# Rotation on the engine that is through first, bias rows first in the queue, attention over half of the dense steps, output products in another order: a four-layer decoder trunk on one core

## The chip, the core and the metric

The kernel runs on one core of a Trainium2 chip. A core has a matrix engine (TensorE, PE in the profile; its weight loads are PEld), two elementwise engines (VectorE, DVE; ScalarE, ACT), a programmable one (GpSimd, POOL) and an engine that here only issues transfers (SyncE, SP). Each works through its own list of instructions in order and waits on semaphores where it needs another's result. The metric is the device time of one execution in microseconds (us).

## The reference

The input is 256 tokens of 1024 numbers. Four layers follow each other. Layer i has a token mixer of kind i mod 3, so the kinds are A, B, C, A, and behind it a SwiGLU block of inner width 2816. Each of the two ends with `x <- LN(alpha*x + f(x))`, in float32.

- Mixer A: attention over a window of 128 tokens, 16 query heads on 4 key heads, with a bias on the projection and on the output, and a learned sink that joins the softmax's denominator.
- Mixer B: three groups of dilated attention with projections of their own, merged by their softmax denominators.
- Mixer C: causal attention in blocks of 256. At 256 tokens there is only the own block, so it is plain causal attention.

All queries and keys are rotated by position in the first 16 of their 64 numbers:

```
x1, x2 = xf[..., :half], xf[..., half:ROT_DIM]
return concatenate([x1 * c - x2 * s, x2 * c + x1 * s, xf[..., ROT_DIM:]], axis=-1)
```

## The kernel before

**Numbers.** Each float32 value is split in two float16 parts, and a product is made of three matmuls: high by high, high by low, low by high (`mm3`, L293 to L295, its three lines name nearly all matmuls of the page). Weights come from memory as float32 in pieces of 128 x 1024 (`raw`, four buffers). ACT makes a piece's high part (`whi`, L229), DVE its low part (`wlo`, L221). Four pieces are one chunk of 512 columns over 1024 rows, and five chunks can be alive at a time. Each of the 412 ring pieces passes this way once.

**One mixer layer.** The tokens are two tiles t of 128. A projection chunk and one token tile take eight steps (k = 0 to 7) of three matmuls into a PSUM bank `acc`, of which there are three. In mixer A a matmul of ones by the row `abias` (L300) adds the bias behind step 4. Then ACT copies the bank to SBUF (`qkv`, L864 in mixer A, L924 in B and C), POOL rotates the first 16 numbers of each head in four operations (L408 to L411), PE transposes the result against `ident` (L304), and ACT and DVE split it into `qkh` and `qkl` (L310, L314). There are 44 such rotations: 6 in each of the layers 0 and 3, 24 in layer 1, 8 in layer 2.

Attention runs in items, each for one token tile and one or two pairs of heads. An item has four kinds of steps: scores on PE with the row minimum on DVE (L521, into `s` and `mn`) and the exponential on ACT (L530); transposes of `s` and the split into `ph` and `pl`; products with the values into `pv`; and, for a group of four heads, the normalisation on DVE (L599, L601, into `oy`), a transpose and the split into `oth` and `otl`. POOL copies the sinks into `s` (L506).

The output product has steps of three matmuls over k for each token tile t and column half h, into one bank per (h, t). Two steps (k = 2q, 2q+1) need the normalised output of four heads. The LayerNorm of a token tile (L653 to L688; POOL takes a power, L680) follows the last product of its two halves, and its result is transposed for the next block.

**What sets the order.** The order of PE, ACT, DVE and POOL is written by a planner that runs while the kernel is built. It holds a time T for every engine and adds an assumed cost for each operation given out. `do(engine, us, dep, ...)` puts an operation into the engine's list when the planner's time has come to `dep`. A weight piece is handed to ACT when the planner believes that it has landed: `T["DMA"] + 2.0` (L257). `drive` (L342) mixes dense steps and attention steps: as long as the done share of attention is below the done share of the first `part` of the dense steps, it takes an attention step whose inputs are there by plan, two at most in a row. `part` is `A_PART`, `B_PART` or `C_PART` (L1064). A dense step of the output product is taken when its heads are collected by plan. SP's order comes from the framework, not from this planner.

**The start.** The eight first loads (x and the four pieces of chunk 0) go out on SP. POOL sends the positions, the sinks and the raw bias `araw`. `bias_parts` (L1022) makes the bias's high part on ACT and its low part on DVE, and POOL sends both as rows into `abias`. Before chunk 1 DVE and ACT make the angles' sine.

Of the kernel before, what the change touches and what calls it, by code (L numbers as in the profile page):

```python
# [18 lines left out]
P = 128  # L19
SEQ, D = 256, 1024  # L20
DEPTH = 4
NT = SEQ // P
# [21 lines left out]
def trunk(ctx, tc, a, out):  # L44
    nc = tc.nc
    ctx.enter_context(tc.manual_schedule(engines={getattr(mybir.EngineType, e) for e in ("PE", "Activation", "DVE", "Pool")}))
    pool = lambda name, bufs, **kw: ctx.enter_context(tc.tile_pool(name=name, bufs=bufs, **kw))
    RING, RAWS = 5, 4
    const = pool("const", 1)
    raw_p = pool("raw", RAWS)  # L50
    w_p = pool("w", RING)
# [32 lines left out]
    big0 = big.tile([P, NFB, SEQ], F16, name="htl").rearrange("p f s -> p (f s)").bitcast(F32)  # L84
    stage = [big0[:, :1024], big0[:, 1024:2048]] + [
        big.tile([P, NK, SEQ], F16, name=n).rearrange("p f s -> p (f s)").bitcast(F32) for n in ("oth", "otl")]
    for h in range(2):
        for t in range(NT):
            nc.sync.dma_start(X[t][:, h * 512:h * 512 + 512], a["x"][t * P:(t + 1) * P, h * 512:h * 512 + 512])
            i = 2 * h + t  # L90
            nc.sync.dma_start(stage[i], a["w_a"][0, 0][:, 1024 * i:1024 * i + 1024])
    nc.gpsimd.dma_start(pos_i, a["positions"].rearrange("(t p) -> p t", p=P))
    nc.gpsimd.dma_start(inv, a["inv"].partition_broadcast(P))
    nc.gpsimd.dma_start(sinks, a["a_sinks"].partition_broadcast(P))
    nc.gpsimd.dma_start(araw, a["a_bias"].rearrange("j (p c) -> p j c", p=P))

# [132 lines left out]
    def feed_one():  # L231

        c = ring["now"]
        if c is None:
            if ring["alive"] == RING:
                return False
            src = next(weights, None)
            if src is None:
                return False
            c = ring["now"] = new_w(*src)  # L240
            loaded.append(c)
        i = c["next"]
        c["next"] += 1
        until(lambda: raws[0] < NEVER)
        T["DMA"] = max(T["DMA"], raws.pop(0)) + 1.45
        raws.append(NEVER)
        slot[0] += 1
        number = slot[0]
        r = raw_p.tile([P, 1024], F32, name="raw")
        nc.sync.dma_start(r, c["src"][:, 1024 * i:1024 * i + 1024])  # L250

        def last(end):

            raws[RAWS - 1 - (slot[0] - number)] = end
        if c["next"] == len(c["ready"]):
            ring["now"] = None
        piece(c, i, r, T["DMA"] + 2.0, last)  # L257
        return True

    slot = [0]  # L260
# [138 lines left out]
    def rope(y, n, t, nh, dep, then):  # L399

        def turn():
            t1 = two.tile([P, 8, ROT], F32, name="rope1")[:, :nh]
            t2 = two.tile([P, 8, ROT], F32, name="rope2")[:, :nh]
            cb = cc[:, t:t + 1, :].to_broadcast([P, nh, ROT])
            sb0 = ss[:, t:t + 1, :h8].to_broadcast([P, nh, h8])
            sb1 = ss[:, t:t + 1, h8:].to_broadcast([P, nh, h8])
            e = nc.gpsimd
            e.tensor_tensor(t1, y[:, :, :ROT], cb, op=OP.mult)  # L408
            e.tensor_tensor(t2[:, :, :h8], y[:, :, h8:ROT], sb0, op=OP.mult)  # L409
            e.tensor_tensor(t2[:, :, h8:], y[:, :, :h8], sb1, op=OP.mult)  # L410
            e.tensor_tensor(y[:, :, :ROT], t1, t2, op=OP.add)  # L411
        do("POOL", 2.2, dep, turn, then)

    def transposed(y, t, n, dst, key):

# [376 lines left out]
    def hbuf(name):  # L792
        return big.tile([P, NFB, SEQ], F16, name=name).rearrange("p f s -> p (f s)").bitcast(F32)

    def finish(li, att, dense, oT, part, may_load=lambda: True, bias=None):

        PS, w = {}, []
        cell, load, half, ln = layer_norm(2 * li, lambda: [two.tile([P, 4, SEQ], F16, name=n) for n in ("qkh1", "qkl1", "qkh2", "qkl2")])

        def o(t):  # L800
            steps = []
            for k, h in [(2 * q + e, h) for q in range(NK // 2) for h in range(2) for e in range(2)]:
                if True:
                    def step(k=k, h=h):
                        if not w:
                            w.extend([next_w(), next_w()])
                        out_steps(PS, oT, NK, w[h], h, t, [k])[0]()
                        if bias is not None and k == 0:
                            add_row(PS[h, t][0], bias[:, 512 * h:512 * h + 512])
                    steps.append((step, lambda k=k: att.collected.get((t, k // 2), NEVER)))  # L810
            return steps
        steps = [(f, None) for f in dense]
        for t in range(NT):
            steps += o(t) + [(lambda t=t: ln(t, PS), None)]
        drive(att, steps, part, len(dense), may_load, load)
        done(2)
        return cell
# [18 lines left out]
    def mixer_a(li, j, cell):  # L836
# [60 lines left out]
            done(2)  # L897
        oT = new_ot()
        dense = chunk_steps(XT, evac(2))
        return finish(li, Attention(items(0) + items(1), oT), dense, oT, A_PART, bias=abias[:, 1536:])  # L900

    def mixer_bc(li, cell, ng):

# [118 lines left out]
    def bias_parts():  # L1022
        nc.scalar.activation(aparts[:, 0], araw, AF.Copy, scale=WS)
        nc.vector.scalar_tensor_tensor(aparts[:, 1], araw, WS, aparts[:, 0], op0=OP.mult, op1=OP.subtract)
        bias_rows(0, nc.gpsimd)

    def first_chunk(XT, evac):

        c = new_w(*next(weights))
        c["next"] = 4  # L1030
        land = [3.6, 5.2, 6.0, 7.6, 8.4, 10.0, 10.8, 12.4]
        spin(6)
        wait(land[0])
        transpose_x(0, XT, 0)
# [15 lines left out]
        for i in (2, 3):  # L1050
            piece(c, i, stage[i], land[1 + 2 * i])
        until(lambda: c["ready"][3] is not None)
        bias_parts()
        do("DVE", 2.2, 0.0, angles)
        T["ACT"] += 2.0
        ring["on"] = True
# [4 lines left out]
            f()  # L1061
        done()

    A_PART, B_PART, C_PART = 0.75, 0.95, 0.85  # L1064
    cell = {"XT": first_xt}
    for li in range(DEPTH):
        kind, j = li % 3, li // 3
# [94 lines left out]
```

## Time and profile before

| what | us |
|---|---|
| median of three runs | 1269.06 |
| lowest and highest of them | 1265.8, 1271.94 |
| the profiled execution's own time | 1272.32 |
| its span, first to last instruction | 1270.5 |
| PE busy | 1240.2 (98%) |
| DVE busy | 878.8 (69%) |
| ACT busy | 668.9 (53%) |
| POOL busy | 131.1 (10%) |

A busy PE isn't a PE at its peak: matmuls overlap, so a row of 0.38 us for 512 columns can follow the one before it by 0.22 us. PEclk is the granted clock as a share of the full 2.4 GHz, over the stretch. In a row of waits, the name behind the arrow is what came last by the profile; where that engine had long been done, it was another.

### The profile page before, as it was taken

How to read it: one execution, taken by the hardware profiler on the slowest of the kernel's cores; microseconds unless marked ns; L12 is line 12 of the kernel's file. 1: busy time of each engine (PE TensorE's matmuls, PEld its weight loads, DVE VectorE, ACT ScalarE, POOL GpSimd, SP SyncE). 2: the span in 40 equal slices, each digit the busy share in tenths (PEclk: the TensorE clock that was granted, in tenths of full speed). 3: DMA queues.
4: the chain of work that ended last, by engine and by line, in shares of the span. 5: the costliest groups of instructions: out<-in, count | busy, mean ns of one | idle time of the engine just before them, and what ended most of it. 6: DMA issues, size and time to landing. Idle time of an engine off the chain costs nothing.

```text
span 1270.5 us, 24604 instructions
## 1 busy us (share of the span) xinstructions
PE 1240.2 (98%) x9990; PEld 828.2 (65%) x9990; DVE 878.8 (69%) x1415; ACT 668.9 (53%) x1102; POOL 131.1 (10%) x270
## 2 busy tenths in 40 slices
PE   7999999999999999999999999999999999999997
PEld 3558888444555555588884445588884455888843
DVE  4798876556676676778665677778665578886632
ACT  4775664336666656546543367546543276465410
POOL 3310000013021203000000122000000132000000
PEclk9999999999999999999999999999999999999999
DMA  6556875546645455357556465457656454676510
GB/s 230 171 166 232 261 253 183 200 149 204 226 135 161 124 180 172 128 166 266 200 183 202 146 218 183 131 165 262 206 183 201 150 164 126 198 258 216 183 51 33
DMA packets 66402, 230.75 MB, mean 182 GB/s; under 512 B 7760, under 2 KB 7792, under 8 KB 66288
## 3 DMA queue, kind: packets, MB, share of 16 engines
q1 hardware_dynamic: 66096, 229.12, 54.5%
q8 instruction: 78, 1.28, 0.4%
q14 instruction: 36, 0.29, 0.1%
q0 software_dynamic: 192, 0.05, 0.0%
HBM read 228.07 MB, written 1.05 MB: 180 GB/s over the span
## 4 chain that ended last, share of the span: by engine, by line
PE 73%; issue 15%; POOL 5%; DVE 4%; ACT 1%; DMA 1%; SPq 0%; POOLq 0%; DVEq 0%; ACTq 0%
PE acc L293 23%; PE acc L294 22%; PE acc L295 22%; PE at L304 3%; POOL qkv L411 2%; POOL rope L408 1%; DVE wlo L221 1%; PE at L544 1%; POOL rope L410 1%; DVE s L521 1%; POOL rope L409 1%; DMA x<-in_x 1%; ACT s L530 0%; DMA raw<-in_w_a 0%; PE pv L295 0%
## 5 line engine op out<-in xcount | busy, mean ns | idle before, releaser
L221 DVE SCALAR_TENSOR_TENSOR wlo<-raw,whi 128x1024 f16<-128x1024 f32 x412 | 495.8, 1229 | 133.6 <-ACT whi L229 129.6
L229 ACT ACTIVATE whi<-raw 128x1024 f16<-128x1024 f32 x412 | 420.6, 1049 | 132.4 <-PE acc L295 54.2
L294 PE MATMUL acc<-xtl,whi 128*128 128x256 f16 (+1 forms) x1664 | 400.6, 256 | 1.1 <-DVE xtl L314 1.1
L295 PE MATMUL acc<-xth,wlo 128*128 128x256 f16 (+1 forms) x1664 | 400.6, 256 | 0.0
L293 PE MATMUL acc<-xth,whi 128*128 128x256 f16 (+1 forms) x1664 | 400.4, 256 | 0.0
L294 PE MATMUL acc<-wlo,xth 128*128 128x512 f16 x480 | 183.6, 382 | 0.8 <-DVE wlo L221 0.6
L293 PE MATMUL acc<-whi,xth 128*128 128x512 f16 x480 | 183.9, 383 | 0.0
L295 PE MATMUL acc<-whi,xtl 128*128 128x512 f16 x480 | 183.5, 382 | 0.0
L295 PEld LDWEIGHTS <-wlo 128*128 128x128 f16 x1664 | 162.8, 98 | 14.7 <-issue 1.5
L294 PEld LDWEIGHTS <-whi 128*128 128x128 f16 x1664 | 162.8, 98 | 13.6
L293 PEld LDWEIGHTS <-whi 128*128 128x128 f16 x1664 | 162.8, 98 | 13.4
L293 PE MATMUL acc<-whi,hth 128*128 128x512 f16 x352 | 133.4, 379 | 0.0
L294 PE MATMUL acc<-wlo,hth 128*128 128x512 f16 x352 | 133.4, 379 | 0.0
L295 PE MATMUL acc<-whi,htl 128*128 128x512 f16 x352 | 133.4, 379 | 0.0
L680 POOL TENSOR_TENSOR mv<-mv,nhalf 128x1 f32<-128x1 f32 x16 | 17.5, 1096 | 829.4 <-DVE mv L677 829.4
L738 ACT ACTIVATE ph<-acc 128x256 f32<-128x256 f32 x88 | 33.4, 379 | 111.2 <-PE acc L295 111.0
L728 DVE SCALAR_TENSOR_TENSOR ph<-ph,acc 128x256 f32<-128x256 f32 x88 | 36.6, 416 | 74.8 <-ACT ph L738 74.8
L295 PEld LDWEIGHTS <-xtl 128*128 128x128 f16 x480 | 47.3, 99 | 59.0 <-issue 3.5
L530 ACT ACTIVATE s<-s,mn 128x257 f32<-128x257 f32 (+5 forms) x128 | 67.1, 526 | 23.7 <-DVE mn L521 22.9
L293 PEld LDWEIGHTS <-xth 128*128 128x128 f16 x480 | 47.2, 98 | 43.1 <-issue 5.1
L294 PEld LDWEIGHTS <-xth 128*128 128x128 f16 x480 | 47.3, 98 | 39.4 <-issue 1.5
L314 DVE TENSOR_TENSOR pl<-at,ph 128x512 f16<-128x512 f32 x76 | 49.5, 658 | 24.9 <-ACT ph L310 24.7
(114 smaller groups left out, 1422.4 us busy)
## 6 DMA issues: line engine op xcount, KB each, us to landing
raw<-in_w_gu SPq DMA_DIRECT2D x176, 512.0 KB, 5.1
raw<-in_w_dn SPq DMA_DIRECT2D x88, 512.0 KB, 4.6
raw<-in_w_b SPq DMA_DIRECT2D x72, 512.0 KB, 4.6
raw<-in_w_c SPq DMA_DIRECT2D x24, 512.0 KB, 5.8
raw<-in_w_a SPq DMA_DIRECT2D x20, 512.0 KB, 5.8
raw<-in_w_ao SPq DMA_DIRECT2D x16, 512.0 KB, 4.8
raw<-in_w_bo SPq DMA_DIRECT2D x8, 512.0 KB, 4.1
raw<-in_w_co SPq DMA_DIRECT2D x8, 512.0 KB, 5.9
```

What stands on the lines that cost most here:

```text
L221: do("DVE", dve(1024), end, lambda: nc.vector.scalar_tensor_tensor(c["lo"][:, s], r, WS, c["hi"][:, s], op0=OP.mult, op1=OP.subtract), lan ...
L229: do("ACT", act(1024), there, lambda: nc.scalar.activation(c["hi"][:, s], r, AF.Copy, scale=WS), low, "w")
L293: nc.tensor.matmul(ps, st[0], mv[0], start=start, stop=False)
L294: nc.tensor.matmul(ps, st[0], mv[1], start=False, stop=False)
L295: nc.tensor.matmul(ps, st[1], mv[0], start=False, stop=stop)
L304: nc.tensor.transpose(ps, src, ident)
L314: nc.vector.tensor_tensor(lo, src, hi, op=OP.subtract)
L411: e.tensor_tensor(y[:, :, :ROT], t1, t2, op=OP.add)
L530: do("ACT", act(n) + 0.17, end, lambda: nc.scalar.activation(s[hh][:, pi], s[hh][:, pi], AF.Exp, bias=mine, scale=-1.0, accum_out=q["l"][: ...
L680: nc.gpsimd.tensor_tensor(mv[:, 3:4], mv[:, 2:3], nhalf, op=OP.pow)
L728: nc.vector.scalar_tensor_tensor(th, th, 1.0, g, op0=OP.add, op1=OP.mult)
L738: do("ACT", act(256), T["PE"] + DRAIN, lambda: nc.scalar.activation(th, g, AF.Tanh, scale=0.5 / WS), lambda at: do("DVE", 0.79, at, gate, ...
```

## The change

The profile's lines are those of the kernel before. Six edits:

1. The rotation runs on DVE or POOL, whichever is through first by the planner's times, with 0.8 us assumed for DVE and 3.3 for POOL (2.2 before).
2. The raw bias is the first transfer on SP. Its parts are made ahead of everything else in `first_chunk`, and its rows go out on SP, not on POOL.
3. The assumed landing of a weight piece is 3.3 us behind T["DMA"], not 2.0 (`LATE`).
4. `A_PART` goes from 0.75 to 0.5, `C_PART` from 0.85 to 0.5; `B_PART` stays at 0.95.
5. In mixer A (`ahead=2`) the output products of the second token tile's first two k-steps, column half 0, stand between those of the first tile, in the third bank; those of half 1 follow behind the first tile's LayerNorm.
6. Mixers B and C keep the order of the output products.

```
-    RING, RAWS = 5, 4
+    RING, RAWS, LATE = 5, 4, 3.3
...
+    nc.sync.dma_start(araw, a["a_bias"].rearrange("j (p c) -> p j c", p=P))
...
-    nc.gpsimd.dma_start(araw, a["a_bias"].rearrange("j (p c) -> p j c", p=P))
...
-        piece(c, i, r, T["DMA"] + 2.0, last)
+        piece(c, i, r, T["DMA"] + LATE, last)
...
-            e = nc.gpsimd
+            e = nc.vector if quick else nc.gpsimd
...
-        do("POOL", 2.2, dep, turn, then)
+
+        quick = max(T["DVE"], dep) + 0.8 <= max(T["POOL"], dep) + 3.3
+        do("DVE" if quick else "POOL", 0.8 if quick else 3.3, dep, turn, then)
...
-    def finish(li, att, dense, oT, part, may_load=lambda: True, bias=None):
+    def finish(li, att, dense, oT, part, may_load=lambda: True, bias=None, ahead=0):
...
+        both = lambda t, q: o(t, 0, (2 * q, 2 * q + 1)) + o(t, 1, (2 * q, 2 * q + 1))
+        last = [(lambda t=t: ln(t, PS), None) for t in range(NT)]
+        if ahead:
+
+            steps += both(0, 0) + both(0, 1) + o(1, 0, range(ahead)) + both(0, 2) + both(0, 3) + last[:1]
+            steps += o(1, 1, range(ahead)) + [f for q in range(ahead // 2, NK // 2) for f in both(1, q)] + last[1:]
+        else:
+            for t in range(NT):
+                steps += [f for q in range(NK // 2) for f in both(t, q)] + last[t:t + 1]
...
-        bias_rows(0, nc.gpsimd)
+        bias_rows(0, nc.sync)
...
+        bias_parts()
         spin(6)
...
-        bias_parts()
         do("DVE", 2.2, 0.0, angles)
...
-    A_PART, B_PART, C_PART = 0.75, 0.95, 0.85
+    A_PART, B_PART, C_PART = 0.5, 0.95, 0.5
```

Three places show what this does to the engines' lists.

The first is SP's queue at the start, from its first transfer on; `htl`, `oth` and `otl` are here the four pieces of chunk 0. Before:

```order
L89 DMA x_102<-in_x 128x512
L91 DMA htl<-in_w_a 128x1024
L89 DMA x_103<-in_x 128x512
...
L91 DMA otl<-in_w_a 128x1024
L250 DMA raw<-in_w_a 128x1024 x2
L887 DMA masks<-in_masks 128x1920
L250 DMA raw<-in_w_a 128x1024 x3
```

Now:

```order
L87 DMA araw<-in_a_bias 128x2x20
L90 DMA x_102<-in_x 128x512
L92 DMA htl<-in_w_a 128x1024
L90 DMA x_103<-in_x 128x512
...
L92 DMA otl<-in_w_a 128x1024
L1026 DMA abias<-aparts 1x128x20 x2
L250 DMA raw<-in_w_a 128x1024
L893 DMA masks<-in_masks 128x1920
```

One transfer moved ahead of the first x tile, and the two bias rows stand ahead of the first ring piece.

The second is ACT and DVE at the end of chunk 0 and the start of chunk 1 in layer 0. `whi_237` and `wlo_238` are the parts of chunk 1, `raw_239` its first piece and `raw_277` (now `raw_293`) its second; `qkv` is the eviction of chunk 0, one for each token tile, and `qkh2_132` the high part of v. ACT before:

```order
L229 ACTIVATE whi_237<-raw_239 128x1024
L864 ACTIVATE qkv_261<-acc_166 128x256
L310 ACTIVATE qkh2_132<-acc_166 128x256
L229 ACTIVATE whi_237<-raw_277 128x1024
L864 ACTIVATE qkv_280<-acc_178 128x256
L229 ACTIVATE whi_237<-raw_295 128x1024
L310 ACTIVATE qkh2_132<-acc_178 128x256
```

ACT now:

```order
L229 ACTIVATE whi_237<-raw_239 128x1024
L870 ACTIVATE qkv_261<-acc_170 128x256
L310 ACTIVATE qkh2_132<-acc_170 128x256
L870 ACTIVATE qkv_277<-acc_182 128x256
L310 ACTIVATE qkh2_132<-acc_182 128x256
L229 ACTIVATE whi_237<-raw_293 128x1024
```

DVE now, the same place:

```order
L221 SCALAR_TENSOR_TENSOR wlo_238<-raw_239,whi_237 128x1024
L408 TENSOR_TENSOR rope1_266<-qkv_261,cc_90 128x64
L409 TENSOR_TENSOR rope2_267<-qkv_261,ss_91 128x4x8
L410 TENSOR_TENSOR rope2_267<-qkv_261,ss_91 128x4x8
L411 TENSOR_TENSOR qkv_261<-rope1_266,rope2_267 128x4x16
L316 SCALAR_TENSOR_TENSOR qkl2_133<-acc_170,qkh2_132 128x256
L891 TENSOR_SCALAR nsink_129<-sinks_106 128x16
L408 TENSOR_TENSOR rope1_282<-qkv_277,cc_90 128x64
L409 TENSOR_TENSOR rope2_283<-qkv_277,ss_91 128x4x8
L410 TENSOR_TENSOR rope2_283<-qkv_277,ss_91 128x4x8
L411 TENSOR_TENSOR qkv_277<-rope1_282,rope2_283 128x4x16
L316 SCALAR_TENSOR_TENSOR qkl2_133<-acc_182,qkh2_132 128x256
```

The second piece's high part moved behind both evictions, and behind the last of these rows on DVE stands its low part. On POOL no rotation is left: its whole list is the setup, 64 copies of sinks and 16 powers.

The third is DVE at the end of attention in layer 3. `s_12637` and `s_12638` are the scores of the last item, and `oy` the normalised output whose heads are an earlier item's. Before:

```order
L314 TENSOR_TENSOR pl_12585<-at_12579,ph_12584 128x512
L314 TENSOR_TENSOR pl_12631<-at_12625,ph_12630 128x512
L521 ISA s_12637,mn_12643<-at_12644,masks_89,nsink_11870 128x256
L521 ISA mn_12643 128x1
L521 ISA s_12638,mn_12643<-at_12645,masks_89,nsink_11870 128x256
...
L599 RECIPROCAL l_12493<-l_12493 128x4
L601 TENSOR_TENSOR oy_12676<-pv_122,l_12493 128x256
```

Now:

```order
L314 TENSOR_TENSOR pl_12568<-at_12562,ph_12567 128x512
...
L601 RECIPROCAL l_12452<-l_12452 128x4
L603 TENSOR_TENSOR oy_12622<-pv_122,l_12452 128x256
L523 ISA s_12637,mn_12643<-at_12644,masks_89,nsink_11870 128x256
L523 ISA mn_12643 128x1
L523 ISA s_12638,mn_12643<-at_12645,masks_89,nsink_11870 128x256
```

The normalisation that stood behind the last item's four reductions stands ahead of them.

## Rows read from the trace of the kernel before

**Rows 1.** The page, part 1: busy time, share of the span, instructions.

```profile
PE 1240.2 (98%) x9990; PEld 828.2 (65%) x9990; DVE 878.8 (69%) x1415; ACT 668.9 (53%) x1102; POOL 131.1 (10%) x270
```

**Rows 2.** PE's waits: total us, times, longest.

```profile
PE acc L300 <- DMA abias<-aparts: 4.6, 1, 4.6
PE at L304 <- POOL qkv L411: 4.0, 5, 2.1
PE pv L293 <- DVE oy L601: 3.5, 2, 2.7
```

**Rows 3.** Stretches: length, busy PE, PEld, DVE, ACT, POOL, clock, DMA share, GB/s.

```profile
20.00:40.00 20.00, 16.63 (x71) 7.29 (x72) 11.54 (x18) 9.30 (x14) 8.99 (x16) 0.91 0.56 184
40.00:60.00 20.00, 19.81 (x165) 11.13 (x164) 14.64 (x47) 16.97 (x48) 6.69 (x22) 0.91 0.48 160
60.00:80.00 20.00, 17.82 (x182) 11.28 (x181) 19.09 (x56) 16.61 (x45) 4.70 (x20) 1.00 0.50 159
...
120.00:200.00 80.00, 80.00 (x779) 72.21 (x777) 61.15 (x85) 48.24 (x69) 0.00 (x0) 1.00 0.77 256
...
760.00:780.00 20.00, 19.12 (x141) 11.17 (x142) 14.74 (x34) 15.06 (x34) 5.73 (x9) 0.91 0.62 207
...
1060.00:1080.00 20.00, 17.34 (x154) 11.22 (x153) 16.52 (x36) 11.62 (x27) 1.09 (x3) 0.91 0.36 117
```

**Rows 4.** Timeline of the start: begin us, us, instruction, [idle before].

```profile
2.12 0.43 SPq L91 DMA_DIRECT2D htl<-in_w_a  x1
...
15.52 0.38 PE L295 MATMUL acc<-whi,xtl 128*128 128x512 f16 x1
...
19.56 1.23 DVE L221 SCALAR_TENSOR_TENSOR wlo<-raw,whi 128x1024 f16<-128x1024 f32 x1 [1.33 <-ACT whi L229]
...
20.54 0.59 PE L300 MATMUL acc<-abias,ones 128*128 128x512 f16 x1 [4.64 <-DMA abias<-aparts]
...
20.91 0.63 PE L293 MATMUL acc<-whi,xth 128*128 128x512 f16 x1
...
25.96 0.38 ACT L864 ACTIVATE qkv<-acc 128x256 f32<-128x256 f32 x1 [6.43 <-PE acc L295]
```

**Rows 5.** Timeline where PE waits for rotations, layers 0 and 2.

```profile
31.77 0.44 PE L304 MATMUL at<-ident,qkv 128*128 128x128 f32 x2 [0.58 <-POOL qkv L411]
...
39.71 0.66 PE L304 MATMUL at<-ident,qkv 128*128 128x128 f32 x4 [2.10 <-POOL qkv L411]
...
758.93 1.35 POOL L411 TENSOR_TENSOR qkv<-rope,rope 128x128 f32<-128x128 f32 x1
...
760.33 0.66 PE L304 MATMUL at<-ident,qkv 128*128 128x128 f32 x4 [1.86 <-DVE mn L521]
```

**Rows 6.** Timeline of one rotation in layer 1, from eviction to transposes.

```profile
294.46 1.22 DVE L221 SCALAR_TENSOR_TENSOR wlo<-raw,whi 128x1024 f16<-128x1024 f32 x1 [0.25 <-ACT whi L229]
294.83 0.60 ACT L924 ACTIVATE qkv<-acc 128x512 f32<-128x512 f32 x1 [0.40 <-PE acc L295]
295.33 1.05 ACT L229 ACTIVATE whi<-raw 128x1024 f16<-128x1024 f32 x1
...
296.63 1.32 POOL L411 TENSOR_TENSOR qkv<-rope,rope 128x128 f32<-128x128 f32 x1
...
298.01 0.66 PE L304 MATMUL at<-ident,qkv 128*128 128x128 f32 x4
```

**Rows 7.** Timeline of small DVE operations: 16 elements a lane.

```profile
20.71 0.17 DVE L1004 COPY ss<-sn 128x16 f32<-128x16 f32 x1
20.78 0.17 DVE L1005 TENSOR_SCALAR ss<-sn 128x16 f32<-128x16 f32 x1
```

**Rows 8.** Groups by line and shape on DVE: count | busy us, mean ns.

```profile
L314 DVE TENSOR_TENSOR pl<-at,ph 128x512 f16<-128x512 f32 x68 | 46.5, 687 | 23.0 <-ACT ph L310 22.8
L314 DVE TENSOR_TENSOR htl<-pl,hth 128x256 f16<-128x256 f32 x88 | 37.0, 421 | 15.4 <-ACT hth L310 15.4
```

**Rows 9.** Timeline at the end of attention in layer 3.

```profile
1064.74 0.21 PE L293 MATMUL pv<-qkh,ph 128*128 128x64 f16 x1 [2.66 <-DVE oy L601]
```

More of the change, by code (lines that the diff above doesn't have):

```diff
@@ L793, in hbuf, with o, step @@
         return big.tile([P, NFB, SEQ], F16, name=name).rearrange("p f s -> p (f s)").bitcast(F32)
-    def finish(li, att, dense, oT, part, may_load=lambda: True, bias=None):
+    def finish(li, att, dense, oT, part, may_load=lambda: True, bias=None, ahead=0):
         PS, w = {}, []
         cell, load, half, ln = layer_norm(2 * li, lambda: [two.tile([P, 4, SEQ], F16, name=n) for n in ("qkh1", "qkl1", "qkh2", "qkl2")])
[L800 to L811, printed above, removed]
-        steps = [(f, None) for f in dense]
-        for t in range(NT):
-            steps += o(t) + [(lambda t=t: ln(t, PS), None)]
+        def o(t, h, ks):
+            def step(k):
+                if not w:
+                    w.extend([next_w(), next_w()])
+                out_steps(PS, oT, NK, w[h], h, t, [k])[0]()
+                if bias is not None and k == 0:
+                    add_row(PS[h, t][0], bias[:, 512 * h:512 * h + 512])
+            return [(lambda k=k: step(k), lambda k=k: att.collected.get((t, k // 2), NEVER)) for k in ks]
+        steps = [(f, None) for f in dense]
+        both = lambda t, q: o(t, 0, (2 * q, 2 * q + 1)) + o(t, 1, (2 * q, 2 * q + 1))
[6 more added lines that the diff above has]
+                steps += [f for q in range(NK // 2) for f in both(t, q)] + last[t:t + 1]
         drive(att, steps, part, len(dense), may_load, load)
@@ L899, in mixer_a @@
         dense = chunk_steps(XT, evac(2))
-        return finish(li, Attention(items(0) + items(1), oT), dense, oT, A_PART, bias=abias[:, 1536:])
+        return finish(li, Attention(items(0) + items(1), oT), dense, oT, A_PART, bias=abias[:, 1536:], ahead=2)
     def mixer_bc(li, cell, ng):
```

## Prediction

> **What bounds the kernel now.** I read the busy shares first [rows 1]: TensorE (PE) is busy 1240.2 of 1270.5 us, VectorE (DVE) 878.8, GpSimd (POOL) 131.1. The number of matmuls is not touched by the change, so the time can only fall by what PE stands idle or runs at half clock. The list of PE's waits comes next [rows 2]: one wait of 4.6 us for the bias rows, five waits of 4.0 us in all for the rotation on POOL, two of 3.5 us for the normalised output `oy`. Last the table of stretches [rows 3]: in four stretches of 20 us the granted clock is 0.91. A stretch at 0.91 has lost 0.09 x 20 = 1.8 us, and each of them holds or follows a PE wait of 2 us or more. In the matmuls themselves: 0.38 us before the bias wait, 0.63 us behind it [rows 4], which is the step from 2.4 to 1.2 GHz after PE stood still for 4.64 us. The stretches of the dense blocks (SwiGLU) run at full clock and with PE busy throughout; nothing is to be had there (80.00 of 80 us from 120 to 200 [rows 3]).
>
> What the change can reach at most is so: bias wait 4.6, rotation waits 4.0, one more of 1.9 at 760.3 us [rows 5], one `oy` wait of 2.7 [rows 9], four times 1.8 of half clock = 7.2. Sum 20.4 us. The wait at 760.3 us is put down to DVE in the row, but the last rotation step on POOL begins at 758.93 and takes 1.35 us, so it ends at 760.28: it belongs to POOL.
>
> **The bias rows.** Before, ScalarE (ACT) makes their high part only after the four first weight pieces, POOL sends the rows, and PE, ready at about 15.7 us, waits until 20.54 [rows 4]. Now the raw bias is the first transfer on SP's queue, its parts are the first work of ACT and DVE, and both rows go out right behind the eight first loads. They should be there before 15.7 us: minus 4.6 us, and minus 1.8 us of half clock behind it. What it costs: one more issue ahead of the first x tile, 0.45 us (0.43 us per issue [rows 4]), which delays everything. Two more issues ahead of the first ring piece (0.9 us) are hidden, since its low part begins only at 19.56 us, behind the sine.
>
> What is late next is the second weight piece of the next chunk. ACT's order shows it: before, its high part stands between the two evictions of the first chunk, now behind both and behind the two high parts of v; on DVE its low part now stands behind two rotations. Worked out: without the wait PE ends the first chunk at 20.7 us (15.7 and seven steps of three matmuls and two bias rows, 23 x 0.213 us, which is 512 columns at 2.4 GHz), the first piece's low part ends at 20.8 (19.56 + 1.23) [rows 4]. The second tile's eviction and its high part of v, 0.38 for 256 columns each [rows 4], end at 21.7, the piece's high part (1.05 [rows 6]) at 22.7. On DVE two rotations and two low parts of v follow on 20.8 and end at 23.4, the low part of the piece at 24.6. PE needs it at 22.5: a new wait of 2.1 us, and half of one half-clock period, 0.9.
>
> **The rotation.** Order shows that of 44 rotations none is left on POOL: the choice of the engine that is through first always falls on DVE. Its price there isn't in the trace, since DVE does no rotation before. From below: operations of 16 elements last 0.17 us [rows 7], so four of them 0.68. From above: the durations for 512 and 256 elements, 0.687 and 0.421 [rows 8], give 1.04 ns per element and 0.155 fixed, so 0.288 for 128 and 0.221 for 64; two of each without overlap are 1.02 us. I take 0.9: the sizes are those of the upper end, but independent operations overlap, as the rows at 20.71 and 20.78 do, which begin 0.07 us apart and last 0.17 each [rows 7].
>
> The Trainium skill speaks against that: VectorE: DVE Perf Modes, section "The DRAIN you can't avoid", says that the next operation doesn't start until the pipe has emptied. By it the rotation would take the full 1.02. The rows at 20.71 and 20.78 do not agree with it for small operations; what follows from it stands among the rivals.
>
> In the first layer 0.6 and 2.1 us of POOL waits go, at 31.77 and 39.71 us, with 1.8 of half clock behind the second [rows 3, 5]. POOL's slow rotations are those beside a running weight conversion (1.35 us for the last step at 758.93 [rows 5]); on DVE they queue behind such a conversion instead.
>
> In layer 1 (24 rotations, 283 to 557 us) I put the term at 0. Order moves the transposes that follow from 15 matmuls behind the end of a chunk to 9 in most cases. In rows 6 they stand at 298.01; six matmuls earlier (6 x 0.213) is 296.73, and the eviction ends at 294.83 + 0.60 = 295.43, which leaves 1.30. The rotation needs 0.9 and two semaphore hops, about 1.0. But DVE is in a conversion until 295.68, 0.25 us behind the eviction's end: 1.25, just within the 1.30. Bounds: minus 1.2 us, if PE waits 0.05 less at each of 24 (POOL's last step ends at 297.95, the transposes begin at 298.01), and plus 6, if it waits a further 0.25 each.
>
> In layer 2 the wait of 1.9, the two of about 0.5 each that are left of rows 2's five, and 1.8 of half clock go: 4.7 us gross.
>
> **Attention over the first half, and the output products.** These move no work in or out. They put about the same DVE work beside less PE work. In layer 0 DVE is busy 19.1 of 20 us from 60 to 80 us [rows 3]: there PE will not get ahead by more than DVE allows. PE reaches the first scores about 7.5 us earlier by the terms above, but DVE has the same work left plus two rotations (1.8 us), and is nearly full. Of DVE's idle time before the scores the start eats some. I take 2.2 us given back by the end of the layer's first LayerNorm.
>
> In layer 3 the `oy` wait of 2.7 at 1064.7 us [rows 9] has a plain cause in the order: the normalisation stands behind four score reductions of the next quad on DVE; now it stands ahead of them, and the products of the second token tile fill PE. With 1.8 of half clock: 4.5 us gross. DVE gets 6 x 0.9 = 5.4 us of rotation there, less one conversion that the planner moves out (1.2 us), in a part where it is busy 16.5 of 20 [rows 3]. I take 2.0 back. In layer 2 the denser attention and the rotations (8 x 0.9 = 7.2 us on DVE) take 1.7 back. Where I am wrong on these three, it is between 0 and the whole gross term.
>
> The later estimate of a landing (3.3 instead of 2.0 us) changes only where a conversion stands in ACT's and DVE's orders. Weights are several chunks ahead in the dense blocks; cost 0 there, bounds 0 and 1 us per layer.
>
> **Sum.** Start: -4.6 -1.8 -0.6 -2.1 -1.8 +0.45 +2.1 +0.9 = -7.5; given back in the first attention +2.2. Layer 1: 0. Layer 2: -4.7 +1.7 = -3.0. Layer 3: -4.5 +2.0 = -2.5. Together -10.8 us, rounded to -10.5 for an unnamed new small wait. The profiled execution took 1272.32 us (span 1270.5 and 1.8 around it), so 1261.8 there; it was 3.3 us above the median of the runs, 1269.06, so I forecast 1258.6 us.
>
> **Rivals.**
> - *DVE gives nearly all back.* For it: the nearly full stretch from 60 us on [rows 3], 44 x 0.9 = 40 us added to 878.8. Against it: over the whole span DVE has 390 us idle. Then only some 3 us stay: 1266 us. Chance 0.22.
> - *Slower: rotations caught behind conversions.* One mechanism: DVE takes its work in order, so a rotation behind a conversion waits up to 1.23 us. It decides from the point at which the conversion ends more than 0.3 us after the eviction; PE then waits at the transposes. If half of the 32 rotations of layers 1 and 2 wait a whole conversion, 16 x (1.23 - 0.3) = 15 us; the start's gain of 7.5 stays, the other layers yield none: 1277 us. For it: rotation steps of 1.32 and 1.35 us on POOL [rows 5, 6] stand beside a conversion on DVE, so the two do meet. Against it: in layer 1, in rows 6, the conversion has 0.25 left. Chance 0.07.
> - *Rotation of 1.02 us.* Without overlap on DVE the 1.25 of layer 1 become 1.37 against 1.30: 24 x 0.07 = 1.7 us, and DVE gets 44 x 0.12 = 5.3 us more, of which I let half show: 4.3 in all, so 1262.9. For it: the durations for 256 and 512 elements [rows 8]; against it: the starts 0.07 us apart [rows 7]. Chance 0.08. This is what the Trainium skill's rule on the drain, named above, would make of it.
> - *All of it.* The new waits don't come, 20 us go: 1249 us. For it: the planner sees DVE's queue and orders by it. Chance 0.08.
> - That the change doesn't do what it says: the bias rows could still be late, since they stand behind 3 MB of loads in the same queue. Then the start's 6.4 us stay and the time is about 1265; I count this within the first rival's chance.
>
> **How the numbers follow.** Forecast 0.55, with its own range 1253 to 1264. With 0.22, 0.07, 0.08 and 0.08 this makes 1. What a measurement of this kernel can tell from no change is 0.5%, so 1262.7 to 1275.4 counts as the same. Faster: 0.53 of the forecast's 0.55, 0.04 of the third rival, 0.08 of the fourth: 0.65. Slower 0.07; same 0.28. The range 1250 to 1267 takes in the first rival and most of the fourth and leaves out under 2 in 10.
>
> **What would show it.** Right: no PE wait for the bias rows and full clock in the first 30 us, a PE wait of about 2 us near 23 us behind a low part of a weight piece; rotation lines on DVE of 0.2 to 0.3 us; no wait for POOL; the stretch near 760 us at full clock; the `oy` wait gone. Wrong: PE waits at the transposes of layer 1 of more than 0.2 us each, clock below 1 in new places, or PE waits in the dense blocks because weights come late.

## The result, and the profile after

The changed kernel takes 1260.09 us (median of 6 runs, 1259.76 to 1263.2) beside 1272.06 us for the kernel before on the same chip: ratio 0.9918, 95% interval 0.9899 to 0.9937. The forecast was 1258.6 us, and "faster by over 0.5%" with a chance of 0.65. The profiled execution took 1259.81 us (span 1258.0) where the sum had said 1261.8.

Part 1 of the page, to be laid beside [rows 1]:

```profile
PE 1233.3 (98%) x9990; PEld 826.3 (66%) x9990; DVE 907.2 (72%) x1591; ACT 669.0 (53%) x1102; POOL 35.3 (3%) x91
```

The number of matmuls is the same, VectorE (DVE) has 28.4 us more, GpSimd (POOL) 95.8 us less. TensorE's (PE) waits, to be laid beside [rows 2] (total us, times, longest):

```profile
PE pv L293 <- DVE oy L603: 3.4, 3, 1.3
PE acc L293 <- DVE x L655: 1.9, 2, 1.0
PE acc L294 <- DVE wlo L221: 1.8, 3, 0.9
PE at L304 <- DMA x<-in_x: 1.6, 3, 0.8
PE pv L295 <- DVE pl L314: 1.5, 2, 1.2
...
PE at L304 <- DVE qkv L411: 1.1, 2, 0.9
```

The waits for the bias rows and for POOL are gone. The wait for `oy` has the same total as before, but is cut in three; line 655 (LayerNorm's first read of a product's bank) and line 221 (low part of a weight piece) are new or longer, and the wait for LayerNorm's output (line 690, 688 before) fell from 1.7 to 0.6 us. The stretches of [rows 3] that ran at half clock, and one that did not:

```profile
20.00:40.00 20.00, 18.05 (x107) 8.68 (x106) 17.59 (x47) 14.82 (x28) 2.06 (x9) 1.00 0.76 250
40.00:60.00 20.00, 19.56 (x183) 11.98 (x184) 16.97 (x47) 16.38 (x42) 2.52 (x16) 1.00 0.38 120
60.00:80.00 20.00, 17.91 (x169) 11.52 (x168) 18.91 (x54) 16.86 (x49) 1.07 (x8) 0.91 0.45 136
...
760.00:780.00 20.00, 18.97 (x165) 11.42 (x162) 15.84 (x51) 14.24 (x40) 0.00 (x0) 1.00 0.41 125
...
1060.00:1080.00 20.00, 19.08 (x171) 12.06 (x168) 18.65 (x30) 9.52 (x12) 1.48 (x1) 1.00 0.59 181
```

All four places of before are at full clock; 60 to 80 us, at full clock before, now has 0.91. So in these two executions three of four half-clock periods are saved, 5.4 us net; the last section shows that other executions have other numbers of them.

To see each layer by itself I cut the span in the dense blocks, where PE is busy throughout, so that a shift of some us moves no wait over a cut. First the kernel before (length, busy PE, PEld, DVE, ACT, POOL, clock, DMA share, GB/s), layers 0 to 3:

```profile
0.00:200.00 200.00, 185.50 (x1689) 136.49 (x1690) 154.04 (x280) 123.22 (x221) 29.21 (x72) 0.98 0.66 219
200.00:600.00 400.00, 399.21 (x3076) 239.25 (x3075) 277.94 (x413) 221.92 (x336) 52.87 (x100) 1.00 0.54 175
600.00:900.00 300.00, 296.70 (x2393) 203.90 (x2392) 210.04 (x339) 159.27 (x268) 23.49 (x36) 0.99 0.57 190
900.00:1240.00 340.00, 336.76 (x2737) 238.72 (x2736) 227.66 (x369) 164.45 (x280) 23.56 (x60) 0.99 0.52 174
```

The same stretches of the changed kernel:

```profile
0.00:200.00 200.00, 190.51 (x1757) 143.05 (x1758) 162.11 (x310) 126.21 (x225) 12.63 (x45) 0.99 0.69 227
200.00:600.00 400.00, 398.62 (x3085) 240.07 (x3083) 295.77 (x511) 224.93 (x338) 4.43 (x4) 1.00 0.54 175
600.00:900.00 300.00, 296.84 (x2412) 205.33 (x2411) 216.02 (x373) 158.82 (x268) 4.68 (x4) 1.00 0.58 191
900.00:1240.00 340.00, 337.58 (x2698) 233.62 (x2696) 224.18 (x383) 159.01 (x272) 11.56 (x36) 1.00 0.51 168
```

Length less busy PE is PE's idle time, before and after: 14.5 and 9.5 us in layer 0, 0.8 and 1.4 in layer 1, 3.3 and 3.2 in layer 2, 3.2 and 2.4 in layer 3. With 1.8 us for each half-clock period (two, none, one, one before; one in layer 0 after) the change is -6.8, +0.6, -1.9 and -2.6, together -10.7 of the span's -12.5. The other 1.8 us are not assigned. Idle time counts only from a matmul's modelled end: one of 0.38 us can be followed after 0.21, so the first 0.17 us of a gap behind it are not seen.

### The profile page after: what moved, and what is told of

Its sections match the earlier page's. It is cut to its first block, busy times and chain, and to the rows that moved or that the text cites. A ratio compares the mean times of both kernels' runs of the same rounds, so it can differ in the third digit from the quotient of the medians.

```text
span 1258.0 us, 24529 instructions
## 1 busy us (share of the span) xinstructions
PE 1233.3 (98%) x9990; PEld 826.3 (66%) x9990; DVE 907.2 (72%) x1591; ACT 669.0 (53%) x1102; POOL 35.3 (3%) x91
## 4 chain that ended last, share of the span: by engine, by line
PE 86%; DVE 6%; ACT 3%; issue 2%; DMA 2%; SPq 0%; POOL 0%; POOLq 0%; DVEq 0%; ACTq 0%
PE acc L293 26%; PE acc L294 26%; PE acc L295 26%; PE at L304 5%; DVE wlo L221 3%; PE at L546 2%; ACT s L532 1%; ACT whi L229 1%; DMA x<-in_x 1%; PE pv L295 1%; PE pv L293 1%; DVE s L523 1%; PE pv L294 1%; DMA raw<-in_w_a 1%; DVE pl L314 0%
## 5 line engine op out<-in xcount | busy, mean ns | idle before, releaser
L310 ACT ACTIVATE hth<-pl 128x256 f16<-128x256 f32 x88 | 36.2, 411 | 57.0 <-DVE pl L731 57.0
L310 ACT ACTIVATE xth<-at 128x512 f16<-128x512 f32 x32 | 19.1, 597 | 81.7 <-PE at L304 81.7
```

What stands on the lines that cost most here:

```text
L310: nc.scalar.activation(hi, src, AF.Copy, scale=1.0 if scale is None else scale)
```

## The experiments

Ratios are to the kernel before, timed on the same chip in the same job; us are medians. The kernel before had medians from 1269.2 to 1272.1 us in these jobs, so ratios count beside the medians, and a difference that only one of the two shows is not settled.

| kernel | us | ratio, interval |
|---|---|---|
| changed kernel | 1260.09 | 0.9918, 0.9899 to 0.9937 |
| without the bias edit | 1266.40 | 0.9969, 0.9957 to 0.9981 |
| without the rotation edit | 1259.48 | 0.9916, 0.9902 to 0.9931 |
| without the new parts | 1265.72 | 0.9960, 0.9947 to 0.9974 |
| without the new product order | 1261.97 | 0.9938, 0.9923 to 0.9954 |
| without the later landing | 1265.62 | 0.9964, 0.9951 to 0.9978 |
| before + bias edit | 1265.54 | 0.9965, 0.9952 to 0.9978 |
| before + rotation on DVE | 1273.59 | 1.0026, 1.0014 to 1.0038 |
| changed, rotation's products twice | 1275.93 | 1.0050, 1.0034 to 1.0067 |
| all on POOL, old landing | 1262.31 | 0.9925, 0.9906 to 0.9944 |
| layers 2, 3 on POOL | 1258.36 | 0.9894, 0.9872 to 0.9917 |
| changed, products filled in | 1261.46 | 0.9925, 0.9905 to 0.9945 |
| layers 2, 3 on POOL, filled in layer 3 | 1260.10 | 0.9927, 0.9907 to 0.9946 |

A caution for all of them: the planner decides by its estimates what comes next, so one altered number reorders many later instructions. Of the versions below, only the bias edit, undone or alone, and the doubled rotation leave PE's order as it was.

**The bias edit undone.** `araw` on POOL's queue, its parts behind the first four weight pieces, rows sent by POOL:

```
-    nc.sync.dma_start(araw, ...)
+    nc.gpsimd.dma_start(araw, ...)
...
-        bias_rows(0, nc.sync)
+        bias_rows(0, nc.gpsimd)
```

> The changed kernel with the bias rows as before (raw bias on POOL's queue, their parts behind the first four weight pieces, rows sent by POOL); TensorE's instruction order is the same as in the changed kernel. Theory A (the terms of the prediction): the wait of 4.6 us and 1.8 us of half clock come back, the 0.45 us of the issue ahead and the wait behind the second weight piece of the next chunk (measured about 1.3 us with its parts) go, so the first chunk's side is 4.5 us longer, of which the nearly full DVE of the first attention hides up to 2.2: 1262 to 1265 us. Rival B (DVE sets the end of the first attention whatever comes before): the same time as the changed kernel, 1260 us within 0.7.

Measured: 6.3 us more, beyond A's upper end; B falls. Its first row of PE's waits:

```profile
PE acc L300 <- DMA abias<-aparts: 4.2, 1, 4.2
```

The wait comes back at 4.2, and 20 to 40 us is at 0.92 again. None of it is hidden by a full DVE.

**The rotation edit undone.** All rotations on POOL, price 2.2 us:

```
-        quick = max(T["DVE"], dep) + 0.8 <= max(T["POOL"], dep) + 3.3
-        do("DVE" if quick else "POOL", 0.8 if quick else 3.3, dep, turn, then)
+        quick = False
+        do("POOL", 2.2, dep, turn, then)
```

> The changed kernel with all rotations on POOL again and with the planner's old price for them (2.2 us). Theory A: PE's waits for POOL come back in layers 0 and 2 (0.6 + 2.1 + 1.8 and 4.7 us), less what DVE gains by 44 rotations of 0.7 to 0.9 us, of which about 4 us had shown: plus 4 to 6 us, 1264 to 1266 us. Rival B (a DVE that is full in the first attention and in layer 3 gives back what POOL's waits cost): no change or faster, 1258 to 1260.5 us. In the trace, A wants waits of TensorE at line 304 for POOL of 3 us or more in all.

Measured: no difference; A falls. The 3 us or more of waits for POOL that A wanted are not there:

```profile
PE at L304 <- POOL qkv L411: 0.9, 1, 0.9
```

So 4.0 us of POOL waits [rows 2] went to 0.9 with the rotations still on POOL; B has the time right, but there was little to give back. By layer (same stretches as above):

```profile
0.00:200.00 200.00, 189.60 (x1750) 142.10 (x1751) 158.38 (x286) 125.95 (x225) 25.76 (x69) 0.99 0.69 227
200.00:600.00 400.00, 399.51 (x3080) 239.56 (x3078) 278.29 (x414) 224.12 (x338) 52.82 (x100) 1.00 0.54 174
600.00:900.00 300.00, 297.54 (x2422) 206.29 (x2420) 210.78 (x341) 158.11 (x266) 20.08 (x36) 1.00 0.58 192
900.00:1240.00 340.00, 338.42 (x2707) 234.08 (x2705) 220.84 (x361) 159.27 (x274) 22.98 (x60) 1.00 0.51 168
```

PE idles 10.4, 0.5, 2.5 and 1.6 us: 0.9 more than the changed kernel in layer 0, and 0.7 to 0.9 less in each of the others.

**The parts undone.** `A_PART, B_PART, C_PART = 0.75, 0.95, 0.85`.

> The changed kernel with attention spread over 0.75 and 0.85 of the dense steps again (layers 0 and 3, and layer 2). Theory A (this part brings the oy wait of layer 3 and its half clock, 4.5 us, less 2.0): plus 2 to 3 us, 1262 to 1263 us, with an oy wait of 2 us or more near 1060 us. Rival B (the oy wait went by the order of the output products and by the rotation, and the denser attention only costs, by the half clock from 60 to 80 us): minus 1 to 2 us, 1258 to 1259 us, and full clock from 60 to 80 us.

Measured: 5.6 us more; A's direction, twice its size. The `oy` wait that A wanted near 1060 us is 1.7 us, not 2 or more. The two layers with the sinks, 0 and 3:

```profile
0.00:200.00 200.00, 188.31 (x1740) 140.76 (x1741) 161.21 (x310) 125.61 (x225) 12.66 (x45) 0.99 0.68 224
...
900.00:1240.00 340.00, 335.39 (x2700) 233.53 (x2699) 226.14 (x386) 161.74 (x276) 11.59 (x36) 1.00 0.50 168
```

PE idles 11.7 (plus 2.2) and 4.6 us (plus 2.2); layer 2 has 3.2 as in the changed kernel. In layer 0 more than half of the longer idle time is behind the attention, where LayerNorm's output is waited for (1.9 us in two at line 690, against 0.6), not where DVE is full. B falls, and 60 to 80 us stays at 0.91, where B wanted full clock.

**The product order undone.** `ahead=0`.

> The changed kernel with the output products of the two tokens tiles one after the other as before. Theory A (this part moves no work and only fills waits): plus 0 to 1.5 us, 1260 to 1261.6 us, with longer waits for oy or pl before the last products of layers 0 and 3. Rival B (its price, the wait of products for a bank that the first tile's LayerNorm still reads, 1.9 us in two waits, is more than it fills): minus 1 to 2 us, 1258 to 1259 us.

Measured: 1.9 us more by medians, 2.5 by ratios, somewhat over A; B falls. PE idles 11.3 us in layer 0 (plus 1.8) and 2.8 in layer 3 (plus 0.3). One place is a wait for the row minimum near 69 us (`mn`, 1.7 us against 0.6), the other the end of layer 0's first LayerNorm:

```profile
107.09 0.63 PE L304 MATMUL at<-ident,x 128*128 128x128 f32 x4 [1.29 <-DVE x L690]
```

In the changed kernel the latter is 0.37 us, at 103.56.

**The landing estimate undone.** `LATE = 2.0`.

> The changed kernel with the old estimate of a weight's landing (2.0 us in place of 3.3). Theory A (prediction: it only moves conversions by places, bounds 0 and 1 us per layer): 1259.5 to 1261.5 us. Rival B (the estimate was needed, a conversion that is put ahead of its landing holds up ACT and DVE in the attentions): plus 2 to 4 us, 1262 to 1264 us, with ACT waiting for DMA.

Measured: 5.5 us more; my price of nothing falls, B holds, above its upper end. One of the places, layer 2, timeline (begin, us, instruction, [idle before]):

```profile
735.77 1.06 ACT L229 ACTIVATE whi<-raw 128x1024 f16<-128x1024 f32 x1 [1.93 <-DMA raw<-in_w_c]
736.73 0.58 ACT L930 ACTIVATE qkv<-acc 128x512 f32<-128x512 f32 x1
736.86 1.23 DVE L221 SCALAR_TENSOR_TENSOR wlo<-raw,whi 128x1024 f16<-128x1024 f32 x1 [1.76 <-ACT whi L229]
738.00 0.28 DVE L408 TENSOR_TENSOR rope<-qkv,cc 128x128 f32<-128x128 f32 x1
...
739.03 0.63 PE L304 MATMUL at<-ident,qkv 128*128 128x128 f32 x4 [1.76 <-DVE qkv L411]
```

ScalarE (ACT) waits 1.93 us for a weight piece that was given out before it landed; the eviction stands behind it in ACT's order, the piece's low part ahead of the rotation in DVE's, and PE waits 1.76 us at the transposes. That is the prediction's slower rival, rotations caught behind conversions; the later landing keeps it away. Over the whole trace PE's waits for the rotation rise from 1.1 to 4.3 us, and those at line 655 from 1.9 to 4.0; the second rise was not followed to its cause.

**The old landing with all rotations on POOL.** Both edits above:

> The run with all rotations on POOL (1259.5 us), with the old estimate of a landing (2.0 us) as well. Theory A (the old estimate hurt the changed kernel by 5.5 us because a conversion given out ahead of its landing stands ahead of a rotation on DVE, as near 737 us of that run; on POOL the rotation is not behind it): at most 1 us above, 1258.5 to 1260.5 us. Rival B (the conversion holds up ACT's evictions and DVE's scores whichever engine rotates): plus 3 to 6 us, 1262.5 to 1265.5 us.

Measured: 2.8 us more than with the later landing by medians, 3.1 by spans, but only 1.1 by ratios; between A and B, so not settled. What is plain is that the waits for POOL come back:

```profile
PE at L304 <- POOL qkv L411: 3.4, 3, 1.2
```

0.9 us with an estimate of 3.3, 3.4 us with 2.0. Four versions, all with the other edits, can now be laid side by side. With the old landing they take 1262.3 us on POOL and 1265.6 on DVE, and the intervals of the ratios do not overlap (0.9906 to 0.9944, 0.9951 to 0.9978). With the later landing they take 1259.5 and 1260.1 us. So DVE is the worse place for the rotation while conversions are given out too early, and no better a place when they are not. The later landing alone, in the kernel before, was not run, and no estimate but 2.0 and 3.3 was.

**Single edits on the kernel before.** The bias edit as in the change; the rotation by `e = nc.vector` and `do("DVE", 0.8, ...)`.

> The kernel before with the bias edit alone (raw bias first in SP's queue, its parts first on ACT and DVE, rows sent by SP); TensorE's order is that of before. Theory A (undoing the edit in the changed kernel cost 6.3 us, so it is worth the wait and the half clock whole, and nothing of it is hidden): 6 us under before, 1265 to 1266.5 us, beside 1271.5. Rival B (it was worth that only with the attention of layer 0 spread thinner; with 0.75 of the dense steps DVE gives it back, by 2.2 us and more): 1267.5 to 1270 us.

Measured: ratio 0.9965, 4.4 us under before, against 6.5 (0.9969 less 0.9918) when undone: between A and B. The 2 us between the two lie within their intervals, so it is not shown that they depend on what else is changed.

> The kernel before with all rotations on DVE, at a planner's price of 0.8 us, and nothing else. Theory A (the prediction's terms for the rotation: 4.5 us in layer 0 and 4.7 in layer 2, less some 4 given back): 1265.5 to 1267.5 us beside 1271.5. Rival B (as the run with the rotations back on POOL in the changed kernel shows no difference, the waits for POOL are paid again as waits for a fuller DVE): 1270.5 to 1272.5 us, without waits for POOL but with about as much wait for DVE.

Measured: 3.3 us slower than before; A falls, and B is too kind. Rows of PE's waits, and a stretch in layer 0:

```profile
PE at L304 <- DVE qkv L411: 3.8, 5, 1.6
PE pv L293 <- DVE oy L601: 3.2, 3, 2.6
```

```profile
60.00:80.00 20.00, 17.28 (x164) 11.28 (x163) 19.07 (x58) 15.72 (x42) 1.53 (x10) 0.85 0.56 185
```

Five waits of 4.0 us for POOL have become five of 3.8 us for DVE, the `oy` wait stays, and where DVE was full before PE stands more and the clock falls to 0.85, a loss of 3.0 us in that stretch.

**The rotation's products twice.** The three products of lines 408 to 410 in a loop of two, sum once; the planner's price is kept.

> The changed kernel with the three products of every rotation done twice on DVE (same results, 132 more DVE operations of about 0.2 us, less by overlap; the planner does not count them, so every engine's order is the same otherwise). Theory A (the rotation's length lies on TensorE's path wherever transposes wait with a slack near 0.05 us, and DVE is full in the attentions): rotations last 0.4 us longer, plus 8 to 15 us, 1268 to 1275 us, some 24 x 0.35 us of it in layer 1. Rival B (DVE has 350 us to spare and the transposes' slack hides it): plus 0 to 3 us, 1260 to 1263 us.

Measured: 15.8 us more, 0.8 beyond A's upper end; B falls. PE waits 20 times for the rotation, 7.4 us in all. One of layer 1 (the lines are one further down):

```profile
290.73 0.29 DVE L409 TENSOR_TENSOR rope<-qkv,cc 128x128 f32<-128x128 f32 x1
...
291.21 0.28 DVE L409 TENSOR_TENSOR rope<-qkv,cc 128x128 f32<-128x128 f32 x1
...
291.62 0.38 PE L295 MATMUL acc<-whi,xtl 128*128 128x512 f16 x1
...
292.24 0.63 PE L304 MATMUL at<-ident,qkv 128*128 128x128 f32 x4 [0.23 <-DVE qkv L412]
```

The second triple adds 0.48 us (291.21 less 290.73). 44 x 0.48 = 21.1 us of DVE work at most (four rotations are half as wide and add less) cost 15.8 us of time: about three quarters lie on the path, though DVE idled 351 us over the span of the changed kernel. The listed 0.23 us is less than what PE loses here. From the begin of the last matmul (291.62) to that of the transposes it is 0.62 us, and 0.21 at the same place of the changed kernel (288.80 to 289.01, rows further down): of the 0.48 us that were added, 0.41 are paid, so the slack was about 0.07. At 41 of the 44 places the transposes follow on another product; there these steps add up to 11.2 us in the changed kernel and 23.7 here, so 12.6 of the 15.8 us arise at the transposes themselves.

**Rotations of layers 2 and 3 on POOL, the others on DVE.** `quick = layer[0] < 2`, price on POOL 2.2.

> The changed kernel with the rotations of layers 2 and 3 (14 of 44) on POOL at the old price, those of layers 0 and 1 on DVE. Theory A (where attention runs, every rotation on DVE is paid on TensorE's path at about its length, where only projections run DVE is the quicker engine; in the run with all rotations on POOL TensorE lost about 1 us less in each of layers 2 and 3): minus 1.5 to 3 us, 1257 to 1258.6 us. Rival B (those differences are chance of the order and fall otherwise when layers 0 and 1 come out as in the changed kernel): 1259.5 to 1261.5 us.

Measured: 1258.36 us, A's range. The interval overlaps that of the changed kernel, so it is not shown to be faster. PE idles 2.2 us in layer 2 and 1.7 in layer 3, 0.9 and 0.7 less than the changed kernel, as with all rotations on POOL.

**More products behind the first tile's LayerNorm**, with all rotations on DVE in layers 0 and 3, then, on the version just told, in layer 3 alone:

```
-            steps += o(1, 1, range(ahead)) + [f for q in range(ahead // 2, NK // 2) for f in both(1, q)] + last[1:]
+            steps += o(1, 0, range(ahead, ahead + 2)) + o(1, 1, range(ahead + 2))
+            steps += [f for q in range(ahead // 2 + 1, NK // 2) for f in both(1, q)] + last[1:]
```

> The changed kernel with four more products put between the first tile's LayerNorm and the products that wait for its bank (the second tile's column half 0, inner blocks 2 and 3). Theory A (the waits for that bank, 1.9 us in two, lie on the path, and 1.3 us of products fill each): minus 1 to 2 us, 1258 to 1259 us, without waits for line 655. Rival B (TensorE is ahead of DVE there in any case, so what it does not wait for the bank it waits for the heads or the LayerNorm): within 0.7 us of 1260.

Measured: 1.4 us more by medians, 0.9 by ratios. The waits for line 655 are gone; in layer 0 a later one of 1.90 us has taken their place, at 95.85 us in the dense block behind LayerNorm, where PE waits for `xtl` of DVE's line 314. A falls; B has the mechanism, though the median lies 0.8 us above its range.

> The version with the rotations of layers 2 and 3 on POOL (1258.4 us), and in layer 3 alone the four more products between the first tile's LayerNorm and the products that wait for its bank. Theory A (in the run that did this in layers 0 and 3 TensorE lost 1.0 us less in layer 3 and 1.2 more in layer 0, so layer 3 alone gains): minus 0.5 to 1.2 us, 1257.2 to 1257.9 us, without the wait for line 655 in layer 3. Rival B (with the rotations of layer 3 on POOL that wait is only 0.2 us, so there is nothing to fill): the same time within 0.5 us, or slower by what the new order disturbs.

Measured: 1260.10 us, 1.7 more than without: A falls, B holds. PE idles 3.0 us in layer 3 against 1.7, and here, too, a wait for `xtl` (1.0 us) comes behind. Its trace also has a half clock from 60 to 80 us, in layer 0, that the trace without lacks, so the whole difference is not the new order's. As far as these two versions show, the wait for the bank cost little on its own, and DVE's chain through LayerNorm sets when PE goes on.

## Why the prediction was right, point by point

The total was right, in part by luck: the terms for the rotation were wrong, and the one I had set to nothing stood for them. By layers, 0 to 3, the forecast was -5.3, 0, -3.0 and -2.5 us, and the traces show -6.8, +0.6, -1.9 and -2.6.

- *Bias rows (-4.6 -1.8).* Right, shown by undoing the edit. The row, without a wait, and the forecast new wait behind it:

```profile
16.49 0.38 PE L300 MATMUL acc<-abias,ones 128*128 128x512 f16 x1
...
23.29 1.22 DVE L221 SCALAR_TENSOR_TENSOR wlo<-raw,whi 128x1024 f16<-128x1024 f32 x1
23.31 0.38 PE L293 MATMUL acc<-whi,xth 128*128 128x512 f16 x1 [0.18 <-ACT whi L229]
...
24.57 0.38 PE L294 MATMUL acc<-wlo,xth 128*128 128x512 f16 x1 [0.88 <-DVE wlo L221]
```

- *The second weight piece (+2.1 +0.9).* The place and the cause are as forecast; it measures 0.18 + 0.88 = 1.1 us, and no half clock follows (1.00 from 20 to 40). I had the low part begin at 23.4 and PE ready at 22.5; it began at 23.29, and PE at about 23.1. PE was later by the x tiles, whose waits are 1.6 us against 0.9; that would be +0.7 for the issue put at +0.45, but in the other traces with the same start these waits are 0.9 to 3.8 us, so the price of the issue can't be read from one.
- *The length of a rotation (0.9).* Right. One in layer 1, to be laid beside [rows 6]:

```profile
287.27 0.60 ACT L930 ACTIVATE qkv<-acc 128x512 f32<-128x512 f32 x1 [0.75 <-PE acc L295]
...
287.90 0.29 DVE L408 TENSOR_TENSOR rope<-qkv,cc 128x128 f32<-128x128 f32 x1
288.11 0.22 DVE L409 TENSOR_TENSOR rope<-qkv,ss 128x64 f32<-128x64 f32 x1
288.25 0.22 DVE L410 TENSOR_TENSOR rope<-qkv,ss 128x64 f32<-128x64 f32 x1
288.50 0.29 DVE L411 TENSOR_TENSOR qkv<-rope,rope 128x128 f32<-128x128 f32 x1
...
288.80 0.38 PE L295 MATMUL acc<-whi,xtl 128*128 128x512 f16 x1
...
289.01 0.60 PE L304 MATMUL at<-ident,qkv 128*128 128x128 f32 x4
```

From 287.90 to 288.79 it is 0.89 us; the four durations add to 1.02. The independent products begin 0.08 us before the one ahead has ended; the sum, which needs them, begins 0.03 behind it. So the full 1.02 of the rival did not come. The Trainium skill, VectorE: DVE Perf Modes, section "The DRAIN you can't avoid", has the next operation wait for the emptied pipe, and adds that a next operation that is not held starts earlier. The prediction left the second half out; in these rows only the dependent operation waits.
- *Layer 1 (0).* Right: plus 0.6 us of PE's idle time. The transposes at 289.01 follow on the last matmul by 0.21, so PE is not held up. The doubled rotation shows how little was spare there: about 0.07 us, close to my 0.05.
- *The rotation's waits in layers 0 and 2 (-0.6 -2.1 -1.8, and -4.7 gross).* This is the step that failed: "the rotation waits 4.0" were booked to the engine. With the engine and its old price put back the time stays, and with the engine alone put on DVE it rises by 3.3 us, with as much waiting for DVE as there was for POOL. What took the waits away in the changed kernel is when conversions are given out: undoing only the later landing costs 5.5 us with the rotation on DVE, and brings POOL's waits from 0.9 to 3.4 us with it on POOL. For the waits this is shown with either engine; for the time it is shown with DVE and not settled with POOL (2.8 us by medians, 1.1 by ratios).
- *The later landing (0, bounds 0 and 1 us per layer).* The other half of the same failure. I looked at the dense blocks, where weights are chunks ahead. It matters in the projections, where a conversion that is given out ahead of its landing holds up the eviction and the rotation behind it.
- *Layer 2 (-3.0).* Two thirds: -1.9. The wait of 1.86 [rows 5] and the half clock went, but two of the three `oy` waits of the list stand here now, 1.0 and 1.3 us.

- *Layer 3 (-2.5).* Right in size: -2.6. The `oy` wait of 2.66 [rows 9] is 1.03 and the clock is full; what was given back stands behind line 655:

```profile
1059.68 0.19 PE L293 MATMUL pv<-qkh,ph 128*128 128x64 f16 x1 [1.03 <-DVE oy L603]
```

- *First attention (+2.2 given back).* Near in size by luck: the half clock from 60 to 80 us is 1.8, which is not the cause that I gave, and another version had none there. That "DVE is nearly full" there would eat the start's gain was wrong, since undoing the bias edit cost 6.3 us. The denser attention and the product order, which I had "move no work in or out", brought 2.2 and 1.8 us in layer 0, much of it at LayerNorm's end.

The sum came out because the later landing's gain, booked at 0, stood where the rotation's was booked; that the two are of like size is luck. The single edits do not add up: undone one by one they cost 6.5, -0.3, 5.3, 2.5 and 5.8 us by ratios (1270 us times the difference to 0.9918), 19.8 in all, for a change of 10.4. All five lean on the one ratio of 0.9918, whose interval moves each by up to 2.4 us; by medians they are 18.7 for 12.0. So some are worth more beside the others than alone; which pairs carry it, beyond the rotation with the landing, is open.

## What to carry to other kernels

A wait that the profile puts down to a slow engine may belong to the order of the work in front of it: try the order with the engine kept, before moving work to an engine that shares its queue with the path. When several edits come together, price the one that "only changes places" with the same care, since it can hold the whole gain of its neighbour. An engine with over a quarter of its span idle can still cost its added work at three quarters, if what is added lies between an eviction and the next engine's turn.

## What was not expected of the hardware

The half clock does not hang on the wait alone. The changed kernel and the version with layers 2 and 3 on POOL have the same PE waits near 70 us, 0.4 us apart. In the changed kernel:

```profile
71.96 0.23 PE L295 MATMUL pv<-qkh,pl 128*128 128x64 f16 x1 [1.24 <-DVE pl L314]
```

```profile
70.00:72.50 2.50, 1.04 (x16) 0.91 (x15) 2.50 (x6) 1.35 (x7) 0.00 (x0) 0.78 0.52 172
72.50:75.00 2.50, 2.50 (x15) 1.97 (x13) 2.40 (x10) 2.37 (x8) 0.00 (x0) 0.54 0.60 206
```

In the other version:

```profile
71.56 0.20 PE L295 MATMUL pv<-qkh,pl 128*128 128x64 f16 x1 [1.24 <-DVE pl L314]
```

```profile
70.00:72.50 2.50, 1.25 (x18) 0.88 (x17) 2.50 (x7) 1.35 (x6) 0.00 (x0) 1.00 0.39 134
72.50:75.00 2.50, 2.15 (x12) 1.25 (x13) 2.40 (x9) 2.50 (x11) 0.00 (x0) 1.00 0.51 188
```

One falls to 1.2 GHz, one stays at 2.4, with a longest wait of 1.24 us in both; my reading that each half-clock stretch holds or follows a wait of 2 us or more was too simple, and the stretch from 760 us, whose wait is 1.86 [rows 5], did not fit it either. The version with the products filled in layer 3 alone has this wait at 71.64 us, 0.08 from the one that kept its clock, and falls (0.91 from 60 to 80 us). The Trainium skill, TensorE: Matmul & The Clock Gate, section "What's actually happening", says that the chip's look at TensorE's activity runs freely and is not started anew with the kernel; these traces agree with that.

Executions of one and the same kernel differ in it too. The version with layers 2 and 3 on POOL had mean granted clocks from 0.996 to 0.999 in four executions, and the traced one is that with 0.999, the fastest (1256.25 us, the others 1258.18 to 1259.57). Eleven executions of the kernel before, beside them, had 0.990 to 0.997; the one at 0.990 took 1275.4 us and the one at 0.997 took 1266.33. So how many half-clock periods a trace holds is partly a draw, and some 1.8 us of a difference between two traces can be that draw. Of the 3.6 us between the two profiled executions above (1259.81 and 1256.25) that much is not the version's merit, and the 5.4 us of saved half clock in the changed kernel hold for the two traces read here.
